# One modulation sum on TensorE, token halves at the start, and three reorderings in an encoder layer on Trainium2

## The chip, the cores and the metric

The kernel runs on one core of a Trainium2 chip. The core has TensorE (PE in the profile; its weight loads are a row of their own, PEld), VectorE (DVE), ScalarE (ACT), GpSimd (POOL) and SyncE (SP), which here only issues DMAs. The metric is the time of one execution on the device in microseconds. Before and after are compared by the medians of several runs.

## The reference

One transformer layer on two sequences of 512 tokens and width 1024, a prompt (batch 0) and a sample (batch 1), each with a condition vector c:

```python
c_act = silu(c)
sh1, sc1, g1, sh2, sc2, g2 = split(c_act @ w_ada + b_ada, 6)
h = rms_norm(x, norm1_g) * (1 + sc1) + sh1
q_a, k_a, v_a, q_r, k_r, v_r, g_r = split(h @ w_in)
o_a = windowed_attention(q_a, k_a, v_a, attn_sink)
o_r = bidirectional_retention(q_r, k_r, v_r, g_r, ret_decay_fwd, ret_decay_bwd)
x = x + g1 * (concat(o_a, o_r) @ w_out)
h = rms_norm(x, norm2_g) * (1 + sc2) + sh2
x = x + g2 * (square(relu(h @ w_mlp1)) @ w_mlp2)
return rms_norm(x, final_g)
```

All arrays are float32. The six parts of `c_act @ w_ada` are the modulations: shift, scale and gate of the mixer and of the MLP.

## The kernel before

**Precision.** A float32 product is made of three products of a shorter type: each operand is split into a high part (a cast on ScalarE) and a low part (a subtraction on VectorE), and high x high, high x low and low x high are added up in one PSUM bank.

**The opening** (lines 1010 to 1210) computes eight column blocks of the input projection for batch 0. It is a list of steps, FRONT, whose order is written out by hand; `pin` keeps each engine to it up to step P.7.0. A name such as P.2.5 calls step_P(2, 5). The steps that the change touches, or that stand around it:

- x.t loads token tile t of x; xp.t loads a pair of chunks of x transposed. sq, nv, nr make the norm factors, xs scales the first 256 columns of a tile by them, xt transposes two chunks of it into the banks pxc, xc copies chunk 1 out.
- tanh and cact make c_act as columns; cbt.i spreads half of one batch's c_act over all partitions by four transposes into the bank pcb_i, and cbc.i copies it to the tile cb.
- trh.s.h loads half h of the row tile of w_ada (transposed) for chunk 0, s = 1 the scale and s = 0 the shift. Ch.s.h multiplies that half by cb and sums along it on VectorE; two halves give one modulation column, mod_a (with norm1_g) or mod_s. tr.k.s and C.k.s are the same for chunk k, whole.
- wi.k loads chunk k of the projection weights, wh.k casts the high part (chunk 0 in halves on VectorE, the others on ScalarE), wl.k subtracts for the low part.
- hh.k makes h of chunk k from x, mod_a and mod_s on ScalarE (function h_high), hm.k makes it once more in full, hl.k subtracts for the low part. rbt, rbc and xn scale the transposed x.
- P.k.c, R.k.c and Q.k.c are the three products of chunk k into the bank of column block c. warm.i.n issues n products of zeros.

**The mixer stages** (lines 556 to 735, 1213 to 1267) run a list of units, one for each 128 columns of weights or quarter of a matrix. After each half of a unit `between` is called: slot n. It runs as many steps of the background modulation sums as digit n of SUMS says (`tick_background`), and at most as many steps of attention blocks and retention heads as digit n of STAGES says (`tick_stage`). At most two of these are active, and each step says how many slots must pass before its next:

```python
        while stages and len(active) < 2:
            kind, start = stages.pop(0)
            active.append([start(), 0, kind])
        for a in active:
            if a[1] <= clock[0] or force:
                wait = next(a[0], "end")
```

`made_through` forces background sums where a later step needs them. The list `later` holds work for a given slot; mixed_0(0) and mixed_0(1), which split the mixer's result for the output projection, stand in it. Within these stages the order on each engine is not pinned.

**The MLP.** The first product goes through 16 pairs of weight tiles (`FirstPair`), seven products p of 12 matmuls each. In this stretch `last_gate` computes the last gate on VectorE: eight chunks, each two batches of two half sums (L262). Before, one call of `tick_background` behind each pair runs the four half sums of a chunk. The second product follows, then the tail, pinned again: it multiplies the last output block tile by tile, adds, norms and stores. `finish_last` (L1483) scales and stores the last tile, rows of two halves of 512 columns, x[0] and x[1], each with a low and a high 256.

## Time and profile before

| | us |
|---|---|
| median of 3 runs | 1084.36 (1084.16 to 1085.21) |
| profiled execution | 1083.92 |
| its span | 1082.1 |
| busy: PE, DVE, ACT, POOL | 1071.3, 866.9, 530.7, 52.2 |
| HBM traffic | 165.46 MB read, 59.53 MB written |

In the views of the profile a row gives the start in microseconds of the span, the duration, the engine, the line of the kernel, the operation, the tiles written and read, and the shapes; in square brackets stands how long the engine had been idle, and what ended that. "x8" is eight such instructions in a row. SPq and ACTq are the queues from which DMAs are issued, and their rows show the issue, not the transfer; a list of issues gives the median time from issue to landing. A row of the stages has, for each engine, the busy time and the number of instructions, then the granted clock of TensorE, the share of the DMA engines that was busy, and GB/s. Matmuls are pipelined, so a record reaches over the start of the next. A row of waits gives who waited for whom, the total, how often, and the longest.

### The profile page before, as it was taken

Reading aid. Unit: us, or ns where it says so; the run is one execution under the profiler, and the core shown is the slowest. Engines: PE = TensorE matmul, PEld = TensorE weight load, DVE = VectorE, ACT = ScalarE, POOL = GpSimd, SP = SyncE. Lnnn points to the kernel's source line nnn. Section 1 sums busy time; section 2 is a strip of 40 time slices with the busy share of each in tenths; the row PEclk is TensorE's granted clock in tenths of the full one; section 3 lists DMA queues with packets and bytes.
Section 4 is the critical chain, followed back from the end, with each engine's and each line's share of the span. In section 5 each row is a group of like instructions: output and inputs, shape, how many; then the busy total and the mean of one; then the engine's idle time right before and its main releaser. Section 6 shows DMA issues by size and latency. Waiting matters only on the chain.

```text
span 1082.1 us, 14072 instructions
## 1 busy us (share of the span) xinstructions
PE 1071.3 (99%) x4998; PEld 885.6 (82%) x4998; DVE 866.9 (80%) x1497; ACT 530.7 (49%) x898; POOL 52.2 (5%) x61
## 2 busy tenths in 40 slices
PE   9999999999999999999999999999999999999997
PEld 6878877778888888898888888888888888888886
DVE  8889999887889885999788787766579654689786
ACT  6577777557663452573333333333354632335342
POOL 2000000000000001010000000000000000003213
PEclk9999999999999999999999999999999999999999
DMA  9965967765555989427454555433973656425504
GB/s 371 409 230 190 341 245 228 231 207 181 195 202 204 320 311 354 154 94 253 157 192 150 186 182 185 176 136 131 329 280 109 193 194 214 175 78 194 195 20 156
DMA packets 88262, 225.92 MB, mean 209 GB/s; under 512 B 8272, under 2 KB 25216, under 8 KB 88192
## 3 DMA queue, kind: packets, MB, share of 16 engines
q1 hardware_dynamic: 87648, 224.30, 59.1%
q8 instruction: 39, 0.64, 0.2%
q0 software_dynamic: 256, 0.55, 0.2%
q14 instruction: 31, 0.25, 0.1%
q10 hardware_dynamic: 288, 0.18, 0.1%
HBM read 165.46 MB, written 59.53 MB: 208 GB/s over the span
## 4 chain that ended last, share of the span: by engine, by line
PE 87%; DVE 7%; ACT 3%; issue 1%; DMA 1%; POOL 0%; ACTq 0%; POOLq 0%; SPq 0%; DVEq 0%
PE x L1412 15%; PE px_None L968 15%; PE y L1412 12%; PE py_None L968 11%; PE po L153 3%; PE po L149 3%; PE po L154 3%; DVE jka_b L200 2%; PE psc L380 2%; PE po L413 2%; PE ppt L406 2%; PE first L1139 1%; PE first L1147 1%; PE first L1143 1%; PE pj_rv L149 1%; PE pj_rv L153 1%
## 5 line engine op out<-in xcount | busy, mean ns | idle before, releaser
L1352 DVE TENSOR_TENSOR uc_l<-ur,uc_h 128x1024 fp32r<-128x1024 f32 x56 | 68.3, 1220 | 52.8 <-ACT uc_h L1352 35.7
L1412 PE MATMUL x<-wc_l,uc_h 128*128 128x512 f32 (+1 forms) x264 | 101.0, 383 | 0.0
L1412 PE MATMUL x<-wc_h,uc_l 128*128 128x512 f32 (+1 forms) x264 | 101.0, 383 | 0.0
L1412 PE MATMUL x<-wc_h,uc_h 128*128 128x512 f32 (+1 forms) x264 | 100.9, 383 | 0.1
L1352 ACT CAST uc_h<-ur 128x1024 fp32r<-128x1024 f32 x56 | 58.8, 1050 | 78.1 <-PE x L1412 27.5
L1412 PE MATMUL y<-wc_h,uc_h 128*128 128x512 f32 x192 | 74.7, 389 | 0.0
L1412 PE MATMUL y<-wc_l,uc_h 128*128 128x512 f32 x192 | 74.7, 389 | 0.0
L1412 PE MATMUL y<-wc_h,uc_l 128*128 128x512 f32 x192 | 74.7, 389 | 0.0
L1352 ACT CAST wc_h<-w 128x1024 fp32r<-128x1024 f32 x48 | 50.4, 1051 | 47.8 <-PE x L1412 24.8
L1352 DVE TENSOR_TENSOR wc_l<-w,wc_h 128x1024 fp32r<-128x1024 f32 x48 | 58.5, 1219 | 17.6 <-ACT wc_h L1352 13.6
L1412 PEld LDWEIGHTS x<-wc_h,uc_h 128*128 128x128 f32 x264 | 49.6, 188 | 10.1 <-issue 0.5
L1412 PEld LDWEIGHTS x<-wc_h,uc_l 128*128 128x128 f32 x264 | 49.6, 188 | 9.8
L1412 PEld LDWEIGHTS x<-wc_l,uc_h 128*128 128x128 f32 x264 | 49.6, 188 | 9.7
L153 PE MATMUL po<-wh_wo,ms 128*128 128x512 f32 x128 | 50.4, 393 | 0.1
L200 DVE CUSTOM_DVE_ANT_0 jka_b<-raw_adat,cb,cols 128x1024 bf16<-128x1024 f32 x40 | 50.1, 1279 | 0.0
L154 PE MATMUL po<-wh_wo,ms 128*128 128x512 f32 x128 | 49.9, 390 | 0.0
L873 ACT CAST wc_s4h<-raw_w 128x1024 fp32r<-128x1024 f32 x16 | 16.8, 1053 | 64.3 <-PE px_None L968 59.7
L1412 PEld LDWEIGHTS y<-wc_h,uc_l 128*128 128x128 f32 x192 | 36.0, 188 | 7.5
L1412 PEld LDWEIGHTS y<-wc_l,uc_h 128*128 128x128 f32 x192 | 36.0, 188 | 7.5
L1412 PEld LDWEIGHTS y<-wc_h,uc_h 128*128 128x128 f32 x192 | 36.0, 188 | 7.4
L390 ACT ACTIVATE st<-st,negm 128x256 f32<-128x256 f32 (+1 forms) x64 | 35.3, 557 | 9.3 <-DVE negm L385 9.3
L874 DVE TENSOR_TENSOR wc_s4l<-raw_w,wc_s4h 128x1024 fp32r<-128x1024 f32 x16 | 19.6, 1224 | 25.0 <-ACT wc_s4h L873 24.4
(399 smaller groups left out, 2960.7 us busy)
## 6 DMA issues: line engine op xcount, KB each, us to landing
ur<-spill SPq DMA_DIRECT2D x56, 512.0 KB, 4.5
raw_adat<-in_w_ada_t_dram SPq DMA_DIRECT2D x40, 512.0 KB, 6.5
raw_w<-in_w_mlp_dram SPq DMA_DIRECT2D x32, 512.0 KB, 3.9
spill<-s SPq DMA_DIRECT2D x64, 256.0 KB, 3.7
w<-in_w_mlp_dram SPq DMA_DIRECT2D x32, 512.0 KB, 4.4
spill<-u SPq DMA_DIRECT2D x48, 256.0 KB, 2.1
x<-in_x_dram SPq DMA_DIRECT2D x16, 512.0 KB, 6.8
raw_ada<-in_w_ada_t_dram SPq DMA_DIRECT2D x14, 512.0 KB, 10.2
```

Source lines behind the costliest of these rows:

```text
L149: nc.tensor.matmul(ps, lhs[1 - late], rhs[late], start=start and low_first, stop=stop and not low_first)
L153: nc.tensor.matmul(ps, lhs[0], rhs[0], start=start and not low_first, stop=False)
L154: nc.tensor.matmul(ps, lhs[late], rhs[1 - late], start=False, stop=stop and low_first)
L200: nc.vector.tensor_tensor_reduce(junk(f"jka_{name}_{sec}_{kc}_{b}"), t, cb[:, b, :], 1.0, bcol[:, sec * KC + kc:sec * KC + kc + 1] if bias ...
L380: nc.tensor.matmul(psc[:, :w], qs[hh][:, isl], k_[:, s, j0 * P:j1 * P], start=(s == 0), stop=(s == 1))
L390: nc.scalar.activation(st[hh][:, :w], st[hh][:, :w], AF.Exp, bias=negm[:, hh:hh + 1], scale=0.125, accum_out=den[:, hh:hh + 1])
L406: nc.tensor.transpose(pt[:, hh * P:(hh + 1) * P], st[hh][:, jj * P:(jj + 1) * P], ident)
L413: nc.tensor.matmul(po, va[:, j0 + jj, g].rearrange("p s e -> p (s e)"), pts[jj][:, s, :], start=(jj == 0 and s == 0), stop=(jj == nj - 1 a ...
L874: nc.vector.tensor_sub(lo, src, f(hi))
L968: self.last = nc.tensor.matmul(bank[:, cs], x[:, k, :], y, start=first and k == 0 and i == 0, stop=last and k == 3 and i == 2, skip_group_ ...
L1352: last_split[:] = [nc.scalar.copy(hi, src), nc.vector.tensor_sub(lo, src, f(hi))]
L1412: nc.tensor.matmul(out, left[n][x][:, i, ts_], right[n][y][:, i, cs], start=first and i == 0 and k == 0, stop=end and i == 1 and k == 2, s ...
```

## The change

- **Opening.** The shift sum of chunk 0 is cut differently: its first half (512 of the 1024 elements of c_act) is no longer a sum on VectorE over a row tile of w_ada, but four matmuls with two moving columns (both batches of c_act) against an untransposed block of w_ada, which a new array w_ada_first holds (step wn loads it, M multiplies, ms adds the bias on ScalarE). The other half continues from it on VectorE as Ch.2. The loads are now, in this order, trh.0 and trh.1 (scale), with wn between them, and trh.2 (shift, second half). cbc.3 moves to ScalarE and cbt.3 shares the bank of cbt.2. Chunk 0 of the weights is loaded in two halves (wih), its h is made in two halves of 256 tokens (hh.0.0, hh.0.1), and its first products run over token halves for column blocks 0 to 5 (P.0.c.0, P.0.c.1). Warming products go from 32 to 23. FRONT has a new order.
- **Mixer stages.** SUMS and STAGES have other digits (sums 71 and 70, steps 161 and 167); mixed_0 comes two slots earlier.
- **Last gate.** last_gate yields after each half sum. It starts behind pair 1 instead of pair 2, and runs one half sum after each of products 3 to 6 of a pair.
- **Last stores.** ScalarE scales x[0] low and issues its store at once; VectorE scales x[1] high and low, which go out in one store from SP, and then x[0] high, stored from SP.

```diff
--- before.py
+++ after.py
@@ last_gate @@
         t = load(0)
-        yield
         for kc in range(KC):
             for b in range(NB):
+                part = small([P, 1], f"gp_{kc}_{b}")
                 for hf in range(2):
-                    if hf == 0:
-                        part = small([P, 1], f"gp_{kc}_{b}")
+                    yield
                     nc.vector.tensor_tensor_reduce(junk(f"jkg_{kc}_{b}_{hf}")[:, :512], t[:, ts_[hf]], rows[b][hf], 1.0,
...
             t = load(kc + 1)
-            yield
+        yield
         store_gates(1)
@@ h_high @@
-    def h_high(b, kc, src, dst):
-        nc.scalar.activation(dst[:, 0, :], src, AF.Identity, bias=mod_s[0][:, kc, b:b + 1], scale=mod_a[0][:, kc, b:b + 1])
+    def h_high(b, kc, src, dst, ts_=slice(0, 512)):
+        nc.scalar.activation(dst[:, 0, ts_], src[:, ts_], AF.Identity, bias=mod_s[0][:, kc, b:b + 1], scale=mod_a[0][:, kc, b:b + 1])
@@ the two strings of the mixer stages @@
-    SUMS = ("110100021002200210200011000010021201221010002110100202120001"
-            "1222011220012010001012221020")
-    STAGES = ("220212301252323112420411231234213022340021420134103304210022"
-              "2012400210421201323242312103")
+    SUMS = ("110100021002200210100001010000021220221100001210210101021111"
+            "0020210220022000200011022212")
+    STAGES = ("420312402044221112430320231324412033430111310143013304210043"
+              "5004300210311301333143312101")
@@ steps of the opening @@
-    def step_trh(s, hf):
-        if hf == 0:
+    def step_trh(q):
+        s, hf = ((1, 0), (1, 1), (0, 1))[q]
+        if q != 1:
             halves[0, s] = r4f(f"raw_ada1_0_{s}")
...
+    def step_wn():
+        one["wn"] = f2("wn")
+        in_order(nc.sync.dma_start(one["wn"], w_ada_first))
+
+    def step_wih(hf):
+        if hf == 0:
+            wi[0] = r4f("raw_wi_0")
+        cs = slice(hf * 512, (hf + 1) * 512)
+        in_order(nc.sync.dma_start(wi[0][:, cs], w_in_first[0][:, cs]))
...
-        wi[kc] = raw_unit(w_in_first[kc], f"wi_{kc}", spare=kc < 2)
+        wi[kc] = raw_unit(w_in_first[kc], f"wi_{kc}", spare=kc == 1)
...
-        banks["cb", i] = (mm_bank if i < 2 else aux_bank)(f"pcb_{i}")
+        if i != 3:
+            banks["cb", i] = (mm_bank if i < 2 else aux_bank)(f"pcb_{i}")
+        else:
+            banks["cb", 3] = banks["cb", 2]
...
-        nc.vector.tensor_copy(dst, banks["cb", i])
+        (nc.scalar.copy if i == 3 else nc.vector.tensor_copy)(dst, banks["cb", i])
...
     def step_xt(t):
-        for c in range(2):
+        for c in (1, 0):
             if t == 0:
-                banks["x", c] = (aux_bank, mm_bank)[c](f"pxc_{c}")
+                banks["x", c] = aux_bank(f"pxc_{c}")
...
+    def step_M():
+        banks["m"] = mm_bank("pm")
+        for kk in range(4):
+            nc.tensor.matmul(banks["m"][:, :NB], one["wn"][:, kk * P:(kk + 1) * P], cact[:, kk, :], start=kk == 0, stop=kk == 3)
+
+    def step_ms():
+        one["C", 0] = small([P, 1], "cs_0")
+        nc.scalar.activation(one["C", 0], banks["m"][:, 0:1], AF.Identity, bias=bcol[:, 0:1])
+
-    def step_Ch(s, hf):
+    def step_Ch(q):
+        s, hf = ((1, 0), (1, 1), (0, 1))[q]
         cs, a_ = slice(hf * 512, (hf + 1) * 512), (mod_s, mod_a)[s][0][:, 0, 0:1]
...
-        nc.vector.tensor_tensor_reduce(junk(f"jka_h_{s}_{hf}")[:, :512], halves[0, s][:, cs], cb[:, 0, cs], 1.0,
-                                       one["C", s] if hf else onep[:, 0:1] if s else bcol[:, 0:1], ALU.mult, ALU.add,
-                                       a_ if hf else one["C", s])
-        if hf and s:
+        nc.vector.tensor_tensor_reduce(junk(f"jka_h_{q}")[:, :512], halves[0, s][:, cs], cb[:, 0, cs], 1.0,
+                                       one["C", s] if hf else onep[:, 0:1], ALU.mult, ALU.add, a_ if hf else one["C", s])
+        if q == 1:
             nc.vector.tensor_tensor(a_, a_, gcol[0][:, 0:1], ALU.mult)
...
-    def step_hh(kc):
-        hm[kc] = r4(f"h_0_0_{kc}"), f2(f"hm_0_0_{kc}")
-        h_high(0, kc, x_chunk(kc), hm[kc][0])
+    def step_hh(kc, hf=None):
+        if not hf:
+            hm[kc] = r4(f"h_0_0_{kc}"), f2(f"hm_0_0_{kc}")
+        h_high(0, kc, x_chunk(kc), hm[kc][0], slice(0, 512) if hf is None else slice(hf * 256, (hf + 1) * 256))
...
-    def step_P(kc, c):
-        if kc == 0:
+    def step_P(kc, c, hf=None):
+        if kc == 0 and not hf:
             open_banks[c] = (mm_bank if c < 3 else aux_bank)(f"first_{c}")
+        ts_ = slice(0, 512) if hf is None else slice(hf * 256, (hf + 1) * 256)
         w, h_, cs = wi[kc], hm[kc][0], slice(c * P, (c + 1) * P)
-        nc.tensor.matmul(open_banks[c], w[0][:, cs], h_[:, 0, :], start=kc == 0, stop=False)
+        nc.tensor.matmul(open_banks[c][:, ts_], w[0][:, cs], h_[:, 0, ts_], start=kc == 0 and not hf, stop=False, skip_group_check=True)
@@ FRONT, the order of the opening by hand @@
-x.0 x.1 warm.0.11 di.0 x.2 di.1 di.2 x.3 bias.0 trh.1.0 bias.1 bias.2 trh.1.1 bias.3 trh.0.0 tanh
-sq.0 cact trh.0.1 cbt.0 cbt.1 nv.0 cbc.0 sq.1 warm.1.4 wi.0 nr.0 cbc.1 cbt.2 xs.0 nv.1 sq.2 tr.1.1
-nr.1 cbt.3 cbc.2 warm.2.3 xs.1 nv.2 sq.3 cbc.3 xt.0 tr.1.0 nr.2 xt.1 warm.3.6 Ch.1.0 xs.2 nv.3
-Ch.1.1 wi.1 nr.3 xt.2 warm.4.3 xs.3 Ch.0.0 xt.3 xp.1 rbt Ch.0.1 xc warm.5.5 wh.0.0 tr.2.1 hh.0
-wh.0.1 hm.0 P.0.0 wl.0 P.0.1 tr.2.0 P.0.2 rbc P.0.3 P.0.4 bias.4 P.0.5 hl.0 P.0.6 bias.5 P.0.7 wi.2
-R.0.0 C.1.1 R.0.1 R.0.2 R.0.3 wh.1 R.0.4 tr.3.1 R.0.5 R.0.6 C.1.0 R.0.7 bias.6 Q.0.0 Q.0.1 Q.0.2
+x.0 x.1 warm.0.11 x.2 di.0 di.1 x.3 di.2 trh.0 bias.0 wn bias.1 bias.2 trh.1 bias.3 trh.2 tanh sq.0
+cact wih.0 cbt.0 wih.1 sq.1 cbt.1 nv.0 cbc.0 nr.0 warm.1.4 cbc.1 tr.1.1 sq.2 nv.1 cbt.2 xs.0 nr.1
+xt.0 cbc.2 warm.2.3 sq.3 nv.2 tr.1.0 nr.2 xs.1 Ch.0 xt.1 cbt.3 xs.2 nv.3 wi.1 M nr.3 cbc.3 Ch.1 xs.3
+xt.2 ms warm.3.1 xp.1 Ch.2 xt.3 rbt xc warm.4.3 wh.0.0 hh.0.0 tr.2.1 wh.0.1 hh.0.1 P.0.0.0 P.0.1.0
+P.0.2.0 hm.0 P.0.3.0 wl.0 P.0.4.0 P.0.5.0 P.0.0.1 tr.2.0 P.0.1.1 P.0.2.1 rbc P.0.3.1 P.0.4.1 P.0.5.1
+P.0.6 bias.4 C.1.1 P.0.7 R.0.0 bias.5 wi.2 R.0.1 R.0.2 R.0.3 R.0.4 hl.0 R.0.5 wh.1 R.0.6 tr.3.1
+R.0.7 C.1.0 Q.0.0 Q.0.1 Q.0.2 Q.0.3 tr.3.0 Q.0.4 Q.0.5 xn.1 hh.1 Q.0.6 Q.0.7 hm.1 wi.3 P.1.0 P.1.1
...
-P.5.6 wh.7 P.5.7 R.5.0 C.6.0 R.5.1 R.5.2 R.5.3 R.5.4 R.5.5 R.5.6 wl.6 hh.6 R.5.7 Q.5.0 Q.5.1 hm.6
+P.5.0 P.5.1 P.5.2 P.5.3 P.5.4 P.5.5 wh.7 hl.5 P.5.6 P.5.7 R.5.0 C.6.0 R.5.1 R.5.2 R.5.3 R.5.4 R.5.5
+R.5.6 wl.6 hh.6 R.5.7 Q.5.0 Q.5.1 hm.6 Q.5.2 Q.5.3 C.7.1 keep.6 Q.5.4 Q.5.5 Q.5.6 Q.5.7 P.6.0 P.6.1
@@ the mixer stages @@
-    later.extend((clock[0] + len(units) * 2 - 2 - k, lambda k=k: mixed_0(k)) for k in (0, 1))
+    later.extend((clock[0] + len(units) * 2 - 4 - k, lambda k=k: mixed_0(k)) for k in (0, 1))
@@ finish_last @@
         nc.scalar.activation(x[0][:, low], x[0][:, low], AF.Copy, scale=r)
+        nc.scalar.dma_start(y[0][:, low], x[0][:, low])
         nc.vector.tensor_scalar(x[1][:, low], x[1][:, low], r, None, ALU.mult)
-        nc.scalar.activation(x[0][:, high], x[0][:, high], AF.Copy, scale=r)
-        for j, cs, engine in ((1, high, nc.sync), (0, low, nc.sync), (1, low, nc.sync), (0, high, nc.scalar)):
-            engine.dma_start(y[j][:, cs], x[j][:, cs])
+        nc.sync.dma_start(y[1], x[1])
+        nc.vector.tensor_scalar(x[0][:, high], x[0][:, high], r, None, ALU.mult)
+        nc.sync.dma_start(y[0][:, high], x[0][:, high])
@@ the first MLP product, pair by pair @@
             elif p in ahead:
                 ahead[p]()
+            if p > 2:
+                tick_background()
         pair.store()
-        if n == 2:
+        if n == 1:
             background.append(last_gate(late))
-        tick_background()
+            tick_background()
@@ arrays on the host @@
+        w_ada_first=ada[:D // 2, :P].reshape(4, P, P).transpose(1, 0, 2).reshape(P, 512),
```

The rest of FRONT differs by moves of single steps within a few places. The two functions step_R and step_Q, and step_P, now pass skip_group_check.

More of the change, by code (lines that the diff above doesn't have):

```diff
@@ L33, in trunk_kernel @@
 @with_exitstack
-def trunk_kernel(ctx, tc, x0, x1, x0_t, x1_t, params, w_ada_t, w_in_first, w_in,
+def trunk_kernel(ctx, tc, x0, x1, x0_t, x1_t, params, w_ada_first, w_ada_t, w_in_first, w_in,
                  w_in_v, w_out, w_mlp1, w_mlp2, final_g, y0, y1):
@@ L1094, in step_xn @@
         x_scale(xt0[t], one["rb"])
-    def step_Ch(s, hf):
-        cs, a_ = slice(hf * 512, (hf + 1) * 512), (mod_s, mod_a)[s][0][:, 0, 0:1]
-        if hf == 0:
-            one["C", s] = small([P, 1], f"cs_{s}")
-        nc.vector.tensor_tensor_reduce(junk(f"jka_h_{s}_{hf}")[:, :512], halves[0, s][:, cs], cb[:, 0, cs], 1.0,
-                                       one["C", s] if hf else onep[:, 0:1] if s else bcol[:, 0:1], ALU.mult, ALU.add,
-                                       a_ if hf else one["C", s])
-        if hf and s:
+    def step_M():
[7 more added lines that the diff above has]
+        s, hf = ((1, 0), (1, 1), (0, 1))[q]
+        cs, a_ = slice(hf * 512, (hf + 1) * 512), (mod_s, mod_a)[s][0][:, 0, 0:1]
+        if q == 0:
+            one["C", 1] = small([P, 1], "cs_1")
+        nc.vector.tensor_tensor_reduce(junk(f"jka_h_{q}")[:, :512], halves[0, s][:, cs], cb[:, 0, cs], 1.0,
+                                       one["C", s] if hf else onep[:, 0:1], ALU.mult, ALU.add, a_ if hf else one["C", s])
+        if q == 1:
             nc.vector.tensor_tensor(a_, a_, gcol[0][:, 0:1], ALU.mult)
@@ L1170, in step_rvs @@
         first_v[kq].loaded([x.rearrange("p (a n) -> p a n", n=512) for x in w])
-    steps = dict(rvl=step_rvl, rvh=step_rvh, rvs=step_rvs, x=step_x, xp=step_xp, trh=step_trh, tr=step_tr, wi=step_wi, tanh=step_tanh,
+    steps = dict(rvl=step_rvl, rvh=step_rvh, rvs=step_rvs, x=step_x, xp=step_xp, trh=step_trh, wn=step_wn, wih=step_wih, M=step_M, ms=step_ms, tr=step_tr, wi=step_wi, tanh=step_tanh,
                  cact=step_cact, cbt=step_cbt, cbc=step_cbc, sq=step_sq, nv=step_nv, nr=step_nr, xs=step_xs, xt=step_xt, xc=step_xc,
@@ new lines, in trunk_kernel @@
+P.3.7 R.3.0 hl.3 R.3.1 R.3.2 wi.6 R.3.3 C.4.0 R.3.4 R.3.5 R.3.6 R.3.7 tr.7.1 Q.3.0 Q.3.1 wl.4 hh.4
+Q.3.2 Q.3.3 Q.3.4 hm.4 Q.3.5 tr.7.0 Q.3.6 C.5.1 Q.3.7 wh.5 P.4.0 P.4.1 P.4.2 wi.7 rvl.0 P.4.3 P.4.4
+hl.4 keep.0 P.4.5 keep.1 keep.2 P.4.6 keep.3 keep.4 P.4.7 C.5.0 R.4.0 R.4.1 R.4.2 R.4.3 R.4.4 R.4.5
+xn.3 hh.5 R.4.6 R.4.7 Q.4.0 hm.5 Q.4.1 Q.4.2 wl.5 Q.4.3 wh.6 Q.4.4 Q.4.5 Q.4.6 Q.4.7 C.6.1 keep.5
+P.5.0 P.5.1 P.5.2 P.5.3 P.5.4 P.5.5 wh.7 hl.5 P.5.6 P.5.7 R.5.0 C.6.0 R.5.1 R.5.2 R.5.3 R.5.4 R.5.5
@@ L1198, in trunk_kernel @@
+R.5.6 wl.6 hh.6 R.5.7 Q.5.0 Q.5.1 hm.6 Q.5.2 Q.5.3 C.7.1 keep.6 Q.5.4 Q.5.5 Q.5.6 Q.5.7 P.6.0 P.6.1
+hl.6 P.6.2 P.6.3 P.6.4 C.7.0 P.6.5 P.6.6 P.6.7 R.6.0 R.6.1 R.6.2 wl.7 hh.7 R.6.3 R.6.4 R.6.5 hm.7
+rvh.0 R.6.6 R.6.7 keep.7 Q.6.0 Q.6.1 hl.7 rvs.0 rvl.1 Q.6.2 Q.6.3 Q.6.4 Q.6.5 Q.6.6 Q.6.7 P.7.0
+R.7.0 Q.7.0 P.7.1 R.7.1 Q.7.1 P.7.2 R.7.2 Q.7.2 P.7.3 R.7.3 Q.7.3 P.7.4 R.7.4 Q.7.4 P.7.5 R.7.5
+Q.7.5 P.7.6 R.7.6 Q.7.6 P.7.7 R.7.7 Q.7.7
     """.split()
```

24 lines of the change are left out of this document (7 added, 17 removed).

## The prediction, made before the change was run

> **What bounds the kernel now.** First the page (span, and the shares of the chain of work that ended last), then the busy times by stage, then the chain in order of time through the opening.
>
> ```profile
> span 1082.1 us, 14072 instructions
> ...
> PE 87%; DVE 7%; ACT 3%; issue 1%; DMA 1%; POOL 0%; ACTq 0%; POOLq 0%; SPq 0%; DVEq 0%
> ```
>
> ```profile
> core 0: us, PE busy (x) PEld busy (x) DVE busy (x) ACT busy (x) POOL busy (x), PEclk, DMA share, GB/s
> ...
> 14.00:54.00 40.00, 39.91 (x176) 33.07 (x177) 36.72 (x55) 22.54 (x31) 0.00 (x0) 1.00 1.03 409
> ...
> 62.00:460.00 398.00, 396.20 (x1907) 327.10 (x1906) 345.10 (x793) 239.56 (x493) 13.71 (x14) 1.00 0.68 236
> ...
> 500.00:1000.00 500.00, 499.93 (x2206) 413.55 (x2205) 369.86 (x476) 195.72 (x249) 8.33 (x2) 1.00 0.54 185
> ```
>
> ```profile
> 12.47 0.75 DVE jka_h L1100
> ...
> 13.26 0.79 ACT h L307
> ...
> 14.09 2.11 PE first L1139 x8
> 16.20 1.81 PE first L1143 x8
> ```
>
> TensorE carries the chain for 87% of the span. From 500 to 1000 us it is never idle (499.93 of 500), so no edit there can gain. The opening waits for the first modulation sums on VectorE, then for the first h on ScalarE; from 14.09 TensorE runs eight 512-column products in each 1.81 us, 0.227 us apiece. But in that stretch DMA is full (1.03 of its engines) and VectorE nearly so (36.72 of 40). Only three places can give time: the start, waits inside the mixer stages (62 to 460), and the last stores.
>
> **The opening, to the first product.**
>
> ```profile
> 2.58 2.73 SPq L1020 DMA_DIRECT2D raw_ada<-in_w_ada_t_dram  x4
> ...
> 5.20 0.20 ACT L1030 ACTIVATE cth<-cols 128x16 f32<-128x16 f32 x1
> ...
> 7.82 1.04 PE L1046 MATMUL pcb<-ident,cact 128*128 128x128 f32 x8
> ...
> 11.13 0.51 ACT L1069 ACTIVATE x<-x,nr 128x256 f32<-128x256 f32 x1 [0.88 <-POOL nr L1064]
> ...
> 12.35 0.59 ACT L1081 COPY xc<-pxc 128x512 f32<-128x512 f32 x1 [0.72 <-PE pxc L1077]
> ...
> 13.15 0.76 DVE L1118 CAST wih<-raw_wi 128x512 fp32r<-128x512 f32 x2
> ```
>
> ```profile
> raw_ada<-in_w_ada_t_dram SPq DMA_DIRECT2D x4, 256.0 KB, 6.8
> ```
>
> ```profile
> 8.00:10.00 2.00, 2.00 (x17) 1.55 (x16) 1.81 (x6) 1.87 (x5) 1.31 (x4) 1.00 1.04 387
> ```
>
> The first of the four half loads lands at 2.58 + 6.8 = 9.4, the others 0.68 apart (256 KB at 387 GB/s): 10.1, 10.7, 11.4. The new order is scale low, w_ada_first, scale high, shift high: the same bytes. So the second scale sum moves from the second landing to the third, 10.7, and ends with its multiply near 11.7. The four two-column products can start at 10.1. No row shows such a product: four 128-column ones take 0.44 (1.04 for eight, 0.11 apart), four 512-column ones 0.9. I take 0.44, the row nearest in width; at either end they are done by 11.0, and step ms stands behind ScalarE's scaling of x.3 (11.13 + 0.51 = 11.64) anyway. With 0.20 for a small activation it ends at 11.84, and the last sum starts at 11.9 instead of 12.47. The copy of the fourth cb half, moved from VectorE to ScalarE, takes some 0.59 (the xc row) and fits the 0.88 that ScalarE waits for nr: nothing; were that cover gone, 0.6 here.
>
> Behind the last sum (12.7) stands one thing that the diff doesn't move: xc, in front of hh.0.0 on ScalarE, 0.11 earlier than now by the swapped transposes, 12.24 to 12.83. Then h for 256 tokens, 0.5 by the 256-column activation, and the first product at 13.4 instead of 14.09. Its weights, half of the 0.76 cast behind the sum, are ready at 13.15. So the start comes **0.7 earlier**; between 0.2 (products and ms late) and 0.9 (xc not in the way).
>
> ```profile
> 1063.93 0.28 PE L1412 MATMUL x<-wc_h,uc_h 128*128 128x256 f32 x1
> ...
> 1066.80 0.40 PE L1412 MATMUL x<-wc_h,uc_h 128*128 128x512 f32 x1
> ```
>
> Between these two starts stand 24 products of 256 columns: 0.12 each. Twelve take 1.44 where six whole ones took 1.36, so the lead is 0.6.
>
> **Where the lead meets the loads.**
>
> ```profile
> 18.46 0.82 ACT L307 ACTIVATE h<-xc,mod_s,mod_a 128x512 fp32r<-128x512 f32 x1 [0.45 <-DVE mod_s L200]
> ...
> 19.67 0.39 PE L1139 MATMUL first<-h,wih 128*128 128x512 f32 x1
> ```
>
> ```profile
> 44.66 1.05 ACT L1118 CAST wih<-raw_wi 128x1024 fp32r<-128x1024 f32 x1 [2.75 <-DMA raw_wi<-in_w_in_first_dram]
> ...
> 45.63 0.81 ACT L307 ACTIVATE h<-xt,mod_s,mod_a 128x512 fp32r<-128x512 f32 x1
> ...
> 46.87 0.39 PE L1139 MATMUL first<-h,wih 128*128 128x512 f32 x1
> ```
>
> At chunk 1, h ends 0.39 before TensorE takes it, but its sums move up too (VectorE loses a half sum and a copy), so the lead passes. At chunk 6 it does not: ScalarE casts wi.7 first, which it gets only when the load lands (2.75 of waiting), and wh.7 still stands ahead of hh.6 in the new order. The load comes off a queue that is full in both windows above, with the same bytes in front of it. So h of chunk 6 cannot end before 46.44, and TensorE has 0.43 to give, less 0.05 for the hand-over, less what two halves of wi.0 cost the queue: 2 x 0.68 against 1.28 (512 KB at 409 GB/s), 0.07. **0.3 of the 0.6 arrives**; the ends are 0 and 0.43.
>
> The Trainium skill, DMA: Bandwidth & Descriptors, section Bandwidth, speaks against halving loads: it says to batch to 1 MiB, and lists 0.95 us for 64 KB and 6.15 for 1 MB. Read linearly, an estimate of 2.0 us for 256 KB, two halves would take 0.6 more than one whole and the opening would end later than now. The trace disagrees: 0.68 a half in a full queue.
>
> **The mixer stages.**
>
> ```profile
> PE pyn L460 <- ACT ryt L456: 1.2, 2, 0.8
> ...
> PE pj_rv L153 <- DVE qs L358: 0.6, 1, 0.6
> PE ppt L406 <- ACT st L398: 0.2, 1, 0.2
> PE pyb L479 <- ACT ryn L474: 0.2, 1, 0.2
> ```
>
> ```profile
> 186.41 0.58 ACT L456 COPY ryt<-py 128x512 f32<-128x512 f32 x1
> ...
> 187.04 0.66 PE L460 MATMUL pyn<-ident,ryt 128*128 128x128 f32 x4 [0.44 <-ACT ryt L456]
> ```
>
> Walking both strings through tick_stage (two active; an attention block waits 2 and 1 slots between its steps, a retention head 1, 2, 1, 1, 1, 1, 2), most changed digits of STAGES change nothing: only steps in slots 8 to 10, 14, 15, 22 to 28, 39, 40, 48, 49, 62 and 63 move, by one slot mostly. In 22 to 28 heads 0 and 1 of batch 0 come to step together, and head 1's copy ryt gets a slot more (12 products, 2.7 us) before its transposes pyn. SUMS drops one sum at slots 18, 22 and 28, partly forced back by made_through, and puts two at 34. The steps mixed_0 come two slots earlier, the same work.
>
> The waits, without pj_rv (which belongs to the evacuation after the opening and moves along), sum to 1.6. A record covers the next start (0.39 long, 0.227 apart), so each hides some 0.16 more: 2.2 in four waits. The 0.44 at 187, which head 1's extra slot meets, and the 0.2 of ppt and of pyb, with a sum less in front, could go: 0.84 + 3 x 0.16 = 1.3. The 0.8 at another head stays: its steps keep their slots, and two sums come shortly before. But the order inside these stages is made from the program's by a scheduler, and 13 moved steps can open waits elsewhere. I take two of those three, **0.9**; the ends are 2.2 gained and 3 lost, a wait like the largest (0.8 + 0.16) for three of the moved groups.
>
> **Last gate and last stores.** The half sums now stand one behind each of the last four products of a pair, where four stood behind the pair; nothing, under the 26% of VectorE that is idle from 500 to 1000 (369.86 busy). Starting a pair earlier is as free.
>
> ```profile
> 1077.54 0.51 ACT L1489 ACTIVATE x2r<-x2r,rf 128x256 f32<-128x256 f32 x1
> ...
> 1077.94 0.35 DVE L1490 TENSOR_SCALAR x2r<-x2r,rf 128x256 f32<-128x256 f32 x1
> ...
> 1078.06 0.90 SPq L1493 DMA_DIRECT2D out_dram<-x2r  x2
> ```
>
> ```profile
> 1079.05 0.41 SPq L1493 DMA_DIRECT2D out_dram<-x2r  x1
> ```
>
> ```profile
> out_dram<-x2r SPq DMA_DIRECT2D x1, 128.0 KB, 2.2
> ```
>
> Three stores queue on SP 0.5 apart; the third issues at 1079.05 and lands at 1081.25. Now ScalarE issues the first of them itself, one SP store takes both halves of x[1] at 1077.94 + 0.35 = 1078.3, and the last half, a further 0.35 on VectorE, is ready at 1078.65 and issues at 1078.8: it lands at 1081.0. **0.25 gained**; ends 0.5 (the ScalarE queue sets the end) and -0.2 (the doubled store holds SP longer).
>
> **Sum.** 0.3 + 0.9 + 0.25, near 1.5. The profiled execution took 1083.92 (span 1082.1 and 1.8 around it), which becomes 1082.4. It stands 0.44 below the median of 1084.36, so the forecast is **1082.9**. A measurement of this kernel tells 0.2%, 2.2 us, from no change: below 1082.2 is faster, above 1086.5 slower.
>
> **The rivals.**
> - All four mixer waits go: 0.3 + 2.2 + 0.25 = 2.8, **1081.6**, or 1081 with what no wait shows. For it: VectorE is busy 345.10 of 398 there, and three of the four lie where sums are deferred. Against: the 0.8 wait's steps keep their slots.
> - Nothing in the mixer moves: 0.55, **1083.8**. That the opening alone does nothing (0) is 0.3 from the forecast.
> - New mixer waits, the side on which it gets slower: heads 0 and 1 step together in slots 22 to 28, each putting its copy and subtract on engines already in demand, and TensorE waits for the second. Three waits of 0.96 less 0.55: **1086.7**; two: 1085.7. It decides where the second head's copy ends later than the 2.7 us of products in front of its consumer.
> - The clock falls back:
>
> ```profile
> 1.24 4.87 PE L1159 MATMUL warm<-idle 128*128 128x512 bf16 x11 [1.24 <-DVE idle L1156]
> ...
> 12.59 1.24 PE L1159 MATMUL warm<-idle 128*128 128x512 bf16 x5
> ```
>
> The same product takes 0.43 in the first row and 0.22 in the second: TensorE starts at half speed for some 4.9 us. The new opening has 23 warming products for 32, the gaps between 9 and 13.4. If speed dropped, a stretch as long as the first at half speed would cost 2.4, 0.6 of it covered by the lead: 1.8 - 0.9 - 0.25, **1085.0**. Against: the transposes and the products stand between the gaps, none over about 1 us. By the Trainium skill, TensorE: Matmul & The Clock Gate, section What's actually happening, it takes an idle window of about 3.4 us to fall back; by that rule it does not happen, and no run here shows a fall-back in mid-kernel.
> - The half sums delay the splits between products: 0.75 of VectorE in each of 8 pairs, if one of the four is not covered, 6.0 less 1.5: **1089**. It decides where VectorE has no idle time inside a product; 369.86 of 500 speaks against.
>
> **How the numbers follow.** Forecast 0.46 (own range 1081.9 to 1083.9: the opening at 0 or the mixer one wait more), all waits 0.22, no mixer gain 0.18, new waits 0.10, clock 0.02, half sums 0.02. Faster: nearly all of the all-waits case (0.20) and a quarter of the forecast, where 0.3 to 0.7 more comes together (0.10), 0.30. Slower: half of the new waits, and the half sums, with some 0.01 of the clock, 0.08. Same: 0.62. The range 1080.9 to 1085.4 leaves out a tenth on each side: below, all waits with both ends of opening and stores; above, the worse new waits.
>
> **What would show it.** Opening: first product near 13.4, a product of chunk 6 near 46.5 with a wait on h in front of it and the load of wi.7 ending near 44.7; if chunk 6 starts at 46.2 the cap is wrong. Mixer: no wait of pyn on ryt near 187, the 0.8 one near 229 still there, TensorE busy over 396.9 of the 398. Stores: last issue 0.25 earlier after the last factor. 500 to 1000 as now. The forecast fails if first products come after 14, if the mixer shows waits that aren't there now, or if VectorE's sums hold a product up after 500.

## The result and the profile after

The changed kernel takes **1089.99 us** (median of 6 runs, 1088.85 to 1091.29) beside 1084.55 for the kernel before (6 runs, 1083.79 to 1085.83): a ratio of 1.0049, 95% interval 1.0036 to 1.0062. It is slower by some 5.4 us, on the other side of the forecast of 1082.9 and outside its range. Its profiled execution took 1089.38, with a span of 1087.6 against 1082.1.

The page, and below it the busy times by stage (columns as before):

```profile
span 1087.6 us, 14052 instructions
...
PE 75%; DVE 13%; DMA 6%; ACT 2%; issue 2%; SPq 1%; POOL 1%; POOLq 0%; DVEq 0%; ACTq 0%
```

```profile
9.00:14.00 5.00, 4.75 (x32) 3.29 (x32) 3.99 (x12) 4.35 (x10) 2.37 (x5) 1.00 1.05 404
...
62.00:460.00 398.00, 394.18 (x1896) 325.29 (x1894) 343.54 (x792) 237.86 (x490) 13.26 (x14) 1.00 0.67 235
...
560.00:680.00 120.00, 118.98 (x520) 96.74 (x519) 96.71 (x165) 40.95 (x62) 0.52 (x1) 1.00 0.52 178
...
500.00:1000.00 500.00, 498.30 (x2191) 410.08 (x2190) 366.18 (x474) 193.24 (x243) 3.01 (x3) 1.00 0.54 185
```

TensorE's share of the chain falls from 87% to 75%, and DMA has 6% of it where it had 1%. TensorE is 2 us less busy in the mixer stages (394.18 of 398 for 396.20), and from 500 to 1000, where it was never idle, 1.6 us are missing (498.30 for 499.93). A busy time flatters, since a record reaches over the next start. So the sizes below come from the starts of the same product in both traces: the first product of the input projection, the first of the retention values (pj_rv), the first of the MLP (px_None), the first of the second MLP product (x).

| kernel | first product | pj_rv | mixer stages, pj_rv to px_None | first MLP product, px_None to x |
|---|---|---|---|---|
| before | 14.09 | 57.75 | 419.80 | 292.49 |
| after | 13.41 | 57.51 | 422.04 | 296.05 |

So **2.2 us are lost in the mixer stages and 3.6 in the first MLP product**; the opening gives 0.24, and after x both kernels run alike up to the tail.

**The opening** went as written. The timeline of the changed kernel from the first scale sum:

```profile
10.26 1.05 PE L1112 MATMUL pm<-cact,wn 128*128 128x2 f32 x8
...
11.62 0.24 ACT L1116 ACTIVATE cs<-pm,cols 128x1 f32<-128x1 f32 x1
...
11.94 0.75 DVE L1123 CUSTOM_DVE_ANT_0 jka_h<-raw_ada,cb,cs 128x512 bf16<-128x512 f32 x1
...
12.79 1.02 ACT L306 ACTIVATE h<-pxc,mod_s,mod_a 128x256 fp32r<-128x256 f32 x2
...
13.41 1.46 PE L1163 MATMUL first<-h,wih 128*128 128x256 f32 x10
```

and at chunk 2 of the weights:

```profile
22.84 1.05 ACT L1140 CAST wih<-raw_wi 128x1024 fp32r<-128x1024 f32 x1 [2.55 <-DMA raw_wi<-in_w_in_first_dram]
23.79 0.81 ACT L306 ACTIVATE h<-xt,mod_s,mod_a 128x512 fp32r<-128x512 f32 x1
...
24.66 0.74 PE L1163 MATMUL first<-h,wih 128*128 128x512 f32 x2
```

The first product starts at 13.41, as forecast. But already at chunk 2 ScalarE waits 2.55 us for the load wi.2 and casts it at 22.84, where the kernel before cast it at 21.66; the h behind that cast holds the products from 24.66 on, and 0.28 of the lead is left behind them. Chunk 7 is cast at 44.56, 0.1 earlier than before, and no product waits there. The load wi.2 lands 2.2 us behind the load in front of it (22.81 and 20.61), where its neighbours land 1.28 apart. One packet of 16 KB of the queue that the profile calls instruction lies there: it starts at 20.32 and takes 1.08 us on one DMA engine. In the kernel before such a packet starts at 23.02, and the load that lands late (25.50, 2.6 behind the one in front of it) is a row of w_ada. That the packet holds the load up is read from this coincidence; no run moves it.

**The mixer stages.** TensorE's four longest waits between 62 and 460 us in the changed kernel (before: pyn for ryt 1.2, ppt 0.2, pyb 0.2):

```profile
PE pj_k L153 <- ACT h L306: 1.1, 1, 1.1
PE pj_k L154 <- DVE h L312: 0.9, 1, 0.9
PE pyb L478 <- ACT ryn L473: 0.8, 1, 0.8
PE pyn L459 <- ACT ryt L455: 0.6, 1, 0.6
```

The wait at 187 and that of ppt are gone, and the one at 229 is down to 0.6, but three new ones stand at 182, 185 and 193 (0.2 before), and two small ones at 220 (0.2) and 414 (0.3). The rows behind the first and the third:

```profile
178.86 1.29 DVE L200 CUSTOM_DVE_ANT_0 jka_b<-raw_adat,cb,onep 128x1024 bf16<-128x1024 f32 x1 [1.18 <-DMA raw_adat<-in_w_ada_t_dram]
...
181.21 0.68 DVE L312 TENSOR_TENSOR h<-hm,h 128x512 fp32r<-128x512 f32 x1
```

```profile
182.98 1.03 PE L459 MATMUL pyn<-ident,ryt 128*128 128x128 f32 x8
```

At 182 TensorE waits for the low part of an h that VectorE makes at 181.21, behind a modulation sum that itself waits 1.18 for its load; ScalarE had finished its input by 179.2. At 185 it waits for the h of the last chunk. That h is not late (ScalarE starts it at 184.49, and at 185.00 in the kernel before): TensorE has less other work in front of the product that needs it. At 193 it waits for the second of two heads that step together: eight transposes pyn stand in a row at 182.98 where each head's four stood apart, and VectorE has the factors of the second head 2.85 us after those of the first (191.93 and 189.08).

**The first MLP product.** TensorE waits here where it did not wait at all; first its weight loads, then its products (480 to 770 us):

```profile
PEld px_None L967 <- DVE u L982: 3.4, 6, 0.7
```

```profile
PE px_None L967 <- DVE u L982: 0.9, 4, 0.3
```

Some 2.9 of the 3.6 us stand in the pairs (pairs 4 to 9 take 19.2 to 19.7 each, 19.04 before). The rest, some 0.6, stands at the hand-over to the second product, where the first product of x starts 1.07 behind the product in front of it (0.45 before) and waits for a u on ScalarE:

```profile
PE x L1437 <- ACT u L988: 0.7, 1, 0.7
```

Why u is late stands upstream. Around one pair, 19 us long, the fourth half sum of a gate chunk (jkg into gm) and the loads of the next pair's weight tiles (raw_w); the kernel before,

```profile
573.72 0.74 DVE L262 CUSTOM_DVE_ANT_0 jkg<-raw_adag,cl,gp 128x512 bf16<-128x512 f32 x1
...
574.50 0.33 SPq L904 DMA_DIRECT2D raw_w<-in_w_mlp_dram  x1
```

and after:

```profile
583.27 0.75 DVE L261 CUSTOM_DVE_ANT_0 jkg<-raw_adag,cl,gp 128x512 bf16<-128x512 f32 x1
...
584.06 0.33 SPq L903 DMA_DIRECT2D raw_w<-in_w_mlp_dram  x1
```

Three buffers named raw go round between w0, w1 and the gate chunk. The load is issued when the fourth sum is done, 9.6 us later than before (2.3 of it because the pair itself starts later, at 562.5 instead of 560.2), and then shares the DMA engines with others (first row before, second after, issues from 574 to 589):

```profile
raw_w<-in_w_mlp_dram SPq DMA_DIRECT2D x2, 512.0 KB, 3.9
```

```profile
raw_w<-in_w_mlp_dram SPq DMA_DIRECT2D x2, 512.0 KB, 5.4
```

The buffer is not all that moved: the order of the issues on SP changed with it. The load of 584.06 now stands behind a store of u that is issued at 580.98 and behind the load of the next gate chunk, issued at 582.82, when VectorE is done with a weight tile (L934, from 582.07). And the load of the second weight tile, which no sum holds, stands behind the stores of s, where it stood at 581.57 in front of them:

```profile
588.45 0.40 SPq L903 DMA_DIRECT2D raw_w<-in_w_mlp_dram  x1
```

**The tail**, after:

```profile
1082.53 0.55 POOL L1502 TENSOR_TENSOR rf<-msf,neghalf 128x1 f32<-128x1 f32 x1 [0.74 <-DVE msf L1498]
...
1084.32 0.40 SPq L1519 DMA_DIRECT2D out_dram<-x2r  x1
```

```profile
out_dram<-x2r SPq DMA_DIRECT2D x1, 128.0 KB, 2.4
```

and the last factor before:

```profile
1076.96 0.55 POOL L1477 TENSOR_TENSOR rf<-msf,neghalf 128x1 f32<-128x1 f32 x1 [0.73 <-DVE msf L1473]
```

The last issue now follows the end of the last factor by 1.24 us (1084.32 - 1083.08), where it was 1.54 (1079.05 - 1077.51). The store that it issues takes 2.4 to land instead of 2.2, so 0.1 is left of 0.3.

### The profile page after: what moved, and what is told of

Its sections match the earlier page's. It is cut to its first block, busy times and chain, and to the rows that moved or that the text cites. A ratio compares the mean times of both kernels' runs of the same rounds, so it can differ in the third digit from the quotient of the medians.

```text
span 1087.6 us, 14052 instructions
## 1 busy us (share of the span) xinstructions
PE 1072.4 (99%) x5001; PEld 884.8 (81%) x5002; DVE 865.9 (80%) x1495; ACT 531.3 (49%) x900; POOL 52.2 (5%) x61
## 2 busy tenths in 40 slices
DMA packets 88262, 225.92 MB, mean 208 GB/s; under 512 B 8272, under 2 KB 24960, under 8 KB 88192
## 4 chain that ended last, share of the span: by engine, by line
PE 75%; DVE 13%; DMA 6%; ACT 2%; issue 2%; SPq 1%; POOL 1%; POOLq 0%; DVEq 0%; ACTq 0%
PE x L1437 15%; PE y L1437 12%; PE px_None L967 7%; PE py_None L967 5%; DMA raw_w<-in_w_mlp_dram 4%; PE po L153 2%; PE po L154 2%; PE po L149 2%; PE psc L379 2%; PE po L412 2%; PE ppt L405 2%; PE pj_rg L153 1%; PE pj_rg L154 1%; PE pj_rg L149 1%; PE first L1163 1%
## 5 line engine op out<-in xcount | busy, mean ns | idle before, releaser
L872 ACT CAST wc_a<-raw_w 128x512 fp32r<-128x512 f32 x32 | 20.0, 624 | 59.5 <-DMA raw_w<-in_w_mlp_dram 52.2
L967 PE MATMUL py_None<-hch,wc_a 128*128 128x512 f32 x120 | 39.6, 389 | 0.0
```

What stands on the lines that cost most here:

```text
L872: nc.scalar.copy(hi, src)
L967: self.last = nc.tensor.matmul(bank[:, cs], x[:, k, :], y, start=first and k == 0 and i == 0, stop=last and k == 3 and i == 2, skip_group_ ...
```

## The experiments

Theory G says that the 3.6 us come from the gate's sums through the buffer; theory M1 that the mixer's loss comes from the sums that the new string SUMS puts off. Beside the first four kernels the kernel before took 1084.33.

**The old gate in the changed kernel** (old loop of `last_gate`, one tick behind each pair):

```diff
-            if p > 2:
-                tick_background()
         pair.store()
-        if n == 1:
+        if n == 2:
             background.append(last_gate(late))
-            tick_background()
+        tick_background()
```

> The changed kernel with the last gate as before: four half sums behind each pair, started behind pair 2; opening, mixer strings and stores as changed. Its pairs 4 to 9 took 19.2 to 19.7 us each where they took 19.04, 3.5 us in all by the offset of the first MLP product's last matmul against its first. Every theory of the gate expects those 3.5 back: about 1.9 us above the kernel before, and 19.04 per pair. If the pairs stay long, the loss in that stretch is not the gate's.

Measured: 1084.89, ratio 1.0007 (0.9998 to 1.0016); the MLP stretch is back at 292.31, the mixer at 421.30. That is 0.6 above the kernel before, not the 1.9 expected.

**The new gate with buffers of its own**, the sums where the change puts them:

```diff
-            return raw_unit(w_ada_t[5, kc], f"adag_{kc}") if kc < KC else None
+            return raw_unit(w_ada_t[5, kc], f"adag_{kc}", True) if kc < KC else None
```

> The changed kernel, half sums between the products as changed, but the gate's tiles of w_ada are loaded into buffers of another kind, not into the three that the weight tiles of the pairs rotate through. Theory G1 (the fourth half sum frees the buffer into which the next pair's first weight tile is loaded; moved behind product 6 it holds that load back some 9 us): pairs back at 19.04, 3.5 us less, about 1.9 above the kernel before. Rival G2 (the sums themselves stand on VectorE in front of splits and bank releases): no gain, about 5.4 above.

Measured: 1085.18, ratio 1.0008 (0.9999 to 1.0017); MLP stretch 292.38. The same half sums between the same products cost nothing once they don't share buffers with the weight tiles. G2 falls. The order on SP is back with it (the two loads of weight tiles of the same pair are issued at 574.31 and 582.61), so no run parts what the held buffer costs by itself from what the order of the issues adds; both come from the sharing. Its stages from 560 to 680, with not one wait of px_None for u left in the view of waits:

```profile
560.00:680.00 120.00, 120.00 (x531) 99.28 (x530) 95.20 (x161) 43.36 (x66) 0.52 (x1) 1.00 0.50 167
```

**Opening and last stores alone**: both strings, `mixed_0` and the gate as before.

> Opening and last stores alone: mixer strings, mixed_0 and last gate as before. By the offsets of the two traces (first product 0.68 earlier, 0.27 of it left at chunk 6, last landing 0.11 nearer to its factor) 0.3 to 0.4 us below the kernel before. A rival in which the earlier opening itself upsets the mixer stages expects it above, by up to 2.

Measured: 1083.85, ratio 0.9996 (0.9987 to 1.0005); mixer 419.72, MLP 292.50. What is good in the change is these two parts, and they are worth less than a measurement can tell.

**The old SUMS in the changed kernel**, all else new:

> The changed kernel with SUMS as before, STAGES as changed. Theory M1 (fewer sums in slots 18 to 28 make the last modulation sums of batch 1, and the loads in front of them, late, and the k projection waits for h): the two waits of pj_k near 182 and 185 go, about 2 us less than the changed kernel, 3.4 above before. Rival M2 (the moved attention and retention steps): they stay, about 5.4 above.

Measured: 1091.4, ratio 1.0068 (1.0055 to 1.008). M1 falls in this form: with the old sums the mixer got worse, not better: 425.10 in its profiled execution, which was the slowest of five (1093.17), and the median too lies above the changed kernel's. A wait of pj_k for h stays, 1.8 us at 185.

So the next theory, M2: the new string STAGES takes retention steps out of the gap in which TensorE waits for the last modulation chunk. Beside the next four the kernel before took 1084.83.

**The new gate alone in the kernel before:**

> The kernel before with the last gate alone changed (one sum per product, begun a pair earlier, its chunk in the buffers of the weight tiles as before). Theory G1 (the fourth half sum of a pair frees the buffer of the next pair's first weight tile, some 9.5 us later than before): pairs 4 to 9 of the first multilayer product take about 19.5 us each instead of 19.04, 3.5 us in all, and everything ahead of them stands as in the kernel before: 1087.9 us, between 1087.4 and 1088.5. Rival G3 (the gate costs the whole 5.1 us that lie between the changed kernel and the one with its old gate, so something outside the pairs goes with it): 1089.4 us. The pair times tell the two apart.

Measured: 1088.33, ratio 1.0034 (1.0022 to 1.0046); MLP stretch 295.70, 3.2 longer, mixer 420.18. By its trace that is G1's size, 0.3 short of it, and the time lies 3.5 above that of the kernel before, as G1 has it.

**The changed kernel with the old gate and the old STAGES:**

> The changed kernel with the old last gate and the old string of attention and retention steps; the new string of sums and the two moved mixer steps stay. Theory M2 (the new order takes the retention steps, which filled TensorE while the last modulation chunk of the second sequence was on its way, out of that gap; the waits of pj_k for h at 182 and 185 us and of the pyb transposes at 192 us are the bill): these waits go, TensorE stands 0.3 to 0.6 us ahead of the kernel before at the first multilayer product, 1083.9 us, between 1083.6 and 1084.3. Rival M1 (the sums that were put off make the last chunk land later: 184.8 us against 184.3 us before): the waits stay, 1084.9 us, as the kernel with the old gate.

Measured: 1088.91, ratio 1.0039 (1.0027 to 1.0051); mixer 423.35. M1 falls, since the waits of pj_k are gone. M2 is right on these waits and wrong on the time: others came (pyb for ryn 0.4 at 186, pyn for ryt 0.8 at 188 and 1.2 at 230, pj_rv 0.6 at 232), and the loss is 2 us larger than with both strings new (421.30). In all the runs, the waits of pj_k and one of pyb of 0.7 to 0.8 near 192 stand in the five traces with the new STAGES and in none with its old first part.

**The same with only the first 48 digits of the old STAGES:**

```diff
-    STAGES = ("420312402044221112430320231324412033430111310143013304210043"
+    STAGES = ("220212301252323112420411231234213022340021420134013304210043"
```

> As the run before, but only the first 48 digits of the string of attention and retention steps are the old ones (up to the second sequence's retention values); the rest is the new string. Theory M2 with its place at k1 and v1, 176 to 193 us: the same as with the whole old string, 1083.9 us, within 0.3 us of it. Rival M3 (the later slots cost as well: the wait of 0.35 us at 414 us, the moved mixer steps): 1084.3 us or more, with the offset against the kernel before growing after 255 us.

Measured: 1088.59, ratio 1.0048 (1.003 to 1.0065); mixer 424.13. Single runs spread widely here (1086.92 to 1093.33). With these digits alone the loss is as large as with the whole old string, so of STAGES the first 48 slots decide; and it comes from the pair of strings, since either one alone is worse than both.

**The new gate with its sums behind the first four products of a pair:**

```diff
-            if p > 2:
+            if p < 4:
                 tick_background()
```

> The changed kernel with the four sums of the last gate put behind the first four products of a pair instead of the last four. Theory G1 (only the end of the fourth sum matters, for the buffer): the fourth sum ends some 8 us earlier in its pair, the first weight tile of the next pair is asked for at about the time of the kernel before, and the pairs take 19.04 us again: 1085.0 us, as with the old gate or with buffers of its own, between 1084.6 and 1085.6. Rival G4 (the sums now stand in front of VectorE's queue before their chunk has landed, which takes 3.9 us from its issue, and hold up the splits behind them): the pairs stay at 19.3 us or more, 1086.5 us or more.

Measured: 1085.83, ratio 1.0008 (1.0 to 1.0017), just above G1's range; MLP stretch 293.57. Pairs 4 to 9 are back at 19.04 (the last at 19.19), as G1 has it; 1.1 of the 3.6 us stays, in the second pair, where VectorE waits for a weight tile:

```profile
509.38 0.47 SPq L903 DMA_DIRECT2D raw_w<-in_w_mlp_dram  x1
...
516.63 0.69 DVE L922 TENSOR_TENSOR ws<-raw_w,raw_w 128x512 f32<-128x512 f32 x1 [3.01 <-DMA raw_w<-in_w_mlp_dram]
```

That load landed 7.2 us after its issue, among stores of 256 KB. It is not what G4 said (sums in front of a chunk that has not landed).

With that, theory V for the mixer: VectorE works through its instructions one by one, and what counts is which of them a modulation sum stands in front of. A retention head needs a normalization on VectorE (BATCH_NORM, then rva and rnb) between two sets of transposes on TensorE (pyn, pyb). The two strings place the sums and the heads' steps against each other. The Trainium skill, PSUM — Partial Sum Buffer, section Engine vs sequencer instructions, calls VectorE's queue strictly first in, first out; the rows below agree. The kernel before took 1084.44 beside the next three.

**The two steps mixed_0 two slots earlier**, in the kernel with the new opening and stores:

> The new opening and the new last stores with the two mixer steps moved two steps earlier, as in the change; both strings of digits and the last gate are the old ones. Theory V (what costs in the mixer is where the sums of the modulation stand in VectorE's order, ahead of the normalizations of the retention heads, whose transposes TensorE waits for; the two strings only make sense together): the moved mixer steps cost nothing, TensorE stays 0.35 us ahead of the kernel before, 1083.9 us, between 1083.5 and 1084.4. Rival X (the mixer steps of the first sequence now run into the retention of the second and bring the waits at 230 and 232 us): 1085.5 us or more.

Measured: 1084.33, ratio 0.9999 (0.999 to 1.0008); mixer 419.96. The moved steps cost 0.2, which is no more than two executions differ by.

**The first 36 digits of the new SUMS** in the kernel with the new opening and stores; they differ in six places:

```diff
-    SUMS = ("110100021002200210100011000010021201221010002110100202120001"
+    SUMS = ("110100021002200210100001010000021220221010002110100202120001"
```

> The new opening and stores, the old last gate, the old string of attention and retention steps, and of the new string of sums only the first 36 digits, which differ in six places (four sums put off, two slots with sums more). Theory V: the sums that were put off stand ahead of the normalizations at 177 to 186 us, so the waits for the heads' transposes come as with the whole new string of sums: TensorE is 1.2 us or more behind the kernel before when pj_k ends and 3 to 4 us behind at 255 us; 1088.0 us, between 1086.5 and 1089. Rival L (the later digits, or the moved mixer steps, bring the cost): within 0.5 us of the kernel before.

Measured: 1089.58, ratio 1.0043 (1.003 to 1.0055); mixer 423.72, 4.0 more than without the six digits. V has the sign and the place, though the time is 0.6 above its range. The place can be read on VectorE. The kernel before:

```profile
177.11 0.30 DVE L464 BATCH_NORM_STATS2 bn<-pyn 128x6 f32<-128x128 f32 x1 [0.22 <-PE pyn L460]
...
180.18 0.16 DVE L467 TENSOR_SCALAR rva<-mv 128x4 f32<-128x4 f32 x1
...
182.49 0.16 DVE L472 SCALAR_TENSOR_TENSOR rnb<-mv,rrs 128x4 f32<-128x4 f32 x1 [0.91 <-POOL rrs L469]
```

With the six digits:

```profile
177.43 1.29 DVE L200 CUSTOM_DVE_ANT_0 jka_b<-raw_adat,cb,onep 128x1024 bf16<-128x1024 f32 x1 [0.66 <-DMA raw_adat<-in_w_ada_t_dram]
...
178.64 0.29 DVE L464 BATCH_NORM_STATS2 bn<-pyn 128x6 f32<-128x128 f32 x1
...
183.02 1.28 DVE L200 CUSTOM_DVE_ANT_0 jka_b<-raw_adat,cb,cols 128x1024 bf16<-128x1024 f32 x1 [0.28 <-DMA raw_adat<-in_w_ada_t_dram]
...
184.23 0.17 DVE L467 TENSOR_SCALAR rva<-mv 128x4 f32<-128x4 f32 x1
...
185.59 0.16 DVE L472 SCALAR_TENSOR_TENSOR rnb<-mv,rrs 128x4 f32<-128x4 f32 x1 [1.19 <-POOL rrs L469]
```

and TensorE's waits with them:

```profile
186.36 0.33 PE L479 MATMUL pyb<-ident,ryn 128*128 128x128 f32 x1 [0.41 <-ACT ryn L474]
188.58 0.65 PE L460 MATMUL pyn<-ident,ryt 128*128 128x128 f32 x4 [0.85 <-ACT ryt L456]
...
230.74 0.66 PE L460 MATMUL pyn<-ident,ryt 128*128 128x128 f32 x4 [1.23 <-ACT ryt L456]
...
232.42 0.50 PE L153 MATMUL pj_rv<-wh_rv,h 128*128 128x512 f32 x1 [0.58 <-ACT wh_rv L122]
```

One sum, which itself waits 0.66 for its load, stands in front of the normalization, a second one in front of rva; the factors of the head are ready 3.1 us later, and the wait for its transposes is followed by another in the next head. By the end of pj_q TensorE is 1.9 behind the kernel before. The larger part, 2.4, comes at 230 to 232 (0.4 is won back later). There two sums (223.75 and 224.96) stand inside the third head's normalization, and its factors come at 228.45, 1.4 later than before. But the digits also changed what V does not speak of: pyn stands behind 12 products of pj_rv, where it stood behind 16, and the cast wh_rv, for which pj_rv waits, comes behind ryn on ScalarE, where it came in front of it. So V is shown at both places, and not that it makes the whole 4.0.

**Two sums moved past a normalization.** If V is all, the kernel before can be improved at 229, its largest wait:

```diff
-    SUMS = ("110100021002200210100011000010021201221010002110100202120001"
+    SUMS = ("110100021002200210100011000010021201023010002110100202120001"
```

> The new opening and stores, everything else old but for two sums, which are put two slots later (digit 36 from 2 to 0, digit 38 from 1 to 3). In the kernel before, three sums of 1.28 us stand on VectorE from 219.03 to 222.65 us, the normalization of the transposes of 220.12 us only starts at 222.77 us, ScalarE gets its factors at 227.31 us, and TensorE waits 0.78 us for the next ryt at 229.34 us. Theory V: without the two sums the normalization starts some 2 us earlier, the wait of 229.34 us goes, 0.8 to 0.9 us are won: TensorE 1.2 us ahead of the kernel before at 255 us, 1083.0 us, between 1082.6 and 1083.6. Rival W (the two sums stand in front of the next normalization instead, or their loads come too late for the ones behind them): the wait comes back further on, 1083.9 us or more.

Measured: 1084.44, ratio 1.0 (0.9991 to 1.0009); mixer 420.11: nothing won. The normalization of the third head on VectorE, the copy of the fourth head on ScalarE and the products before its transposes on TensorE:

```profile
220.77 0.30 DVE L464 BATCH_NORM_STATS2 bn<-pyn 128x6 f32<-128x128 f32 x1
```

```profile
225.92 0.60 ACT L456 COPY ryt<-py 128x512 f32<-128x512 f32 x1
```

```profile
224.43 0.39 PE L153 MATMUL pj_rv<-wh_rv,h 128*128 128x512 f32 x1
224.66 0.39 PE L154 MATMUL pj_rv<-wh_rv,h 128*128 128x512 f32 x1
224.88 0.39 PE L153 MATMUL pj_rv<-wh_rv,h 128*128 128x512 f32 x1
226.57 0.66 PE L460 MATMUL pyn<-ident,ryt 128*128 128x128 f32 x4 [1.30 <-ACT ryt L456]
```

VectorE did what V said: the normalization starts at 220.77 instead of 222.77, and ryt at 225.92 instead of 228.69. But the transposes pyn stand behind 3 products of pj_rv, where they stood behind 16 in the kernel before. Nothing in the edit touches TensorE: where the order is not pinned, the program's scheduler sets it, and it drew the transposes forward too. The wait of 0.78 became one of 1.30, and neither V's gain nor W's new wait behind it is what happened.

**The same with those transposes kept back** (the digit 37 of STAGES from 4 to 0); beside it the kernel before took 1084.48:

```diff
-    STAGES = ("220212301252323112420411231234213022340021420134103304210022"
+    STAGES = ("220212301252323112420411231234213022300021420134103304210022"
```

> As the run with the two sums put two slots later, and the transposes of the fourth head kept back (digit 37 of the other string from 4 to 0): in the order of the instructions on TensorE they now stand behind 12 products of pj_rv instead of 3 (16 in the kernel before). Theory P (the sums moved as meant, but the program's scheduler, which orders each engine where nothing pins it, drew the transposes forward by 13 products, so that the wait stayed): the products begin at 224.4 us, 12 of them end at 227.1 us, ryt is there at 226.5 us, so the wait of 1.46 us at 226.57 us goes and no wait takes its place: TensorE 1.2 us ahead of the kernel before at 255 us, 1083.2 us, between 1082.7 and 1083.8. Rival Q (every digit reshuffles what follows, and a wait comes back elsewhere): no more than 0.5 us ahead at the first product of the multilayer part, 1084.0 us or more.

Measured: 1084.01, ratio 0.9995 (0.9986 to 1.0004); mixer 420.54. The transposes run at 227.64 with no wait, as P says, and the last retention value product of the second sequence starts at the kernel before's time; two other waits take it all back, as Q says:

```profile
237.37 0.50 PE L380 MATMUL psc<-ks,qs 128*128 128x256 f32 x2 [0.84 <-DVE mx L382]
```

```profile
357.54 0.50 PE L153 MATMUL po<-wh_wo,ms 128*128 128x512 f32 x1 [0.59 <-DVE rg L364]
```

No version that is clearly faster than the kernel before came out: the kernel with the new opening and stores alone, and this one, lie 0.5 us below it, inside their intervals.

## Why the prediction was wrong, step by step

- **Opening: right, with the cap in the wrong place.** First product 13.4 forecast, 13.41 measured; the four two-column products took 1.05 where 0.44 was taken and 0.9 was the upper end, but end at 11.3, ahead of the scaling that ms stands behind, as the step said. 0.3 of the lead was to arrive, limited by the load of chunk 7 at chunk 6; 0.24 to 0.28 did, limited by the load of chunk 2. That the two sizes agree is luck. The table and the rows above show it, and the run of opening and stores alone keeps it to the end. The rule of the Trainium skill (DMA: Bandwidth & Descriptors, Bandwidth) by which the halves would cost 0.6 does not hold in this full queue: they land 0.67 us each behind the load in front of them, 1.34 for both, where the whole took 1.28.
- **Clock: right.** With 23 warming products the granted clock is 1.00 between 9 and 14 us, as the Trainium skill's rule has it (TensorE: Matmul & The Clock Gate, What's actually happening). That column also reads 1.00 in the first 5 us, where warming products stand 0.43 apart; the better witness is that the two at 12.69 stand 0.21 apart.
- **Last stores: mis-sized.** The issue moved as reckoned (0.3 earlier for 0.25), but the term took over the old 2.2 to landing; it is 2.4 here, behind a store twice as large, and 0.1 is left. Whether the larger store is the reason no run shows.
- **Mixer: wrong sign.** Three things were in the step. Which waits there were, and that the one at 187 and that of ppt would go: right. That the mixed_0 steps are free: right. What failed is "0.9, two of those three": it was read from the waits that the old order shows, taken one by one, with the slot as the measure of the distance between a copy and its transposes ("12 products, 2.7 us"). The run with two sums moved shows that slots do not fix that distance: the scheduler changed it from 16 products to 3 without an edit of STAGES. The six digits of SUMS, which the step counted as "a sum less in front", cost 4.0 us with the old STAGES; its list of the changed digits left out slots 25 and 35 and the 27 from 36 on. The rival "new mixer waits" (0.10) had the right sign, and with three waits of 0.96 (2.9) came near the 2.2 of the profiled execution; the three kernels with the same mixer and another gate lost 1.1 to 1.5 (420.88, 421.29 and 421.30 against 419.80). Its mechanism, two heads that step together, shows in one of the three new waits, the 0.8 at 193; the other two are waits for h, which no rival named.
- **Last gate: the largest error.** "Nothing, under the 26% of VectorE that is idle" named the wrong cover. VectorE's time was not what the sums used up: with other buffers they cost nothing (292.38). What they hold until the fourth sum ends is the buffer that the next pair's first weight tile needs. The term put at nothing is thus the one that failed: the release of the buffer, and with it the loads of the next pair, moved with the fourth sum, 7.3 us later in the pair. It cost 3.5 us where the gate alone was changed and 3.6 in the trace of the whole change. The rival of the half sums had the place and even the time (1089), but for 0.75 us of VectorE a pair, and at 0.02; that the time fits is luck.

What stays open: which digit each of the three new waits of the mixer follows from where both strings are new, why the wait at the hand-over to the second product stands in the changed kernel and not with the gate alone, and why the sizes differ between 1.1 and 2.2 us in four executions of the same mixer. The time between the changed kernel and the one with the old gate is 5.1 us, of which 3.7 stand in the MLP stretch and 0.7 in the mixer stretch of these two traces; the rest is within the spread of single runs. That is 1.6 more than the 3.5 which the gate costs alone, and no run shows why.
